# A mixture-of-experts diffusion block on one core: experts' results weighted at their eviction, residual tiles loaded ahead, layer 1's attention norm applied untransposed

## Chip, cores and metric

The kernel runs as one program on one core of a Trainium2 chip. The metric is the device time of one execution in microseconds. It is given as the median of three runs; the profile comes from one further execution.

## The reference, cut to what matters

Two layers work on 1024 latent tokens and 256 context tokens of width 1024, all in float32. Each layer has an attention part and a mixture of 32 experts, of which each token uses two. Only the parts that the change touches are shown.

```python
for i in range(DEPTH):                                   # 2 layers
    sh_a, sc_a, gt_a, sh_f, sc_f, gt_f = jnp.split(mod, 6, axis=-1)     # one row each for latents (modc for context)
    h  = _modulate(_rmsnorm(x, g_attn[i]), sh_a, sc_a)   # rmsnorm(x) * g * (1 + sc) + sh
    hc = _modulate(_rmsnorm(xc, g_attn[i]), shc_a, scc_a)
    q, k, v = _split_qkv(h, w_qkv[i])
...
    y = _hier_moe(tokens, ...)      # out[token] = sum over its 2 experts of w_buf * ((silu(xe @ w_gate) * (xe @ w_up)) @ w_down)
    x = x + gt_f * y[:b * n].reshape(b, n, d)
    if not last:
        xc = xc + gtc_f * y[b * n:].reshape(xc.shape)
return _rmsnorm(x, g_final)
```

In the last layer only the latents go through the experts.

## The kernel before, in words

Tokens are handled in tiles of 128, one token per partition: 8 latent tiles and 2 context tiles. Each layer runs in stages, one after another: `keys` (attention norm, keys and values), `queries`, attention (`attention` in layer 0, `dense` in layer 1), `project` (output projection, residual, second norm, routing) and `moe` (the experts). After layer 1 comes `final`. PE is TensorE, DVE is VectorE, ACT is ScalarE, POOL is GpSimd and SP is SyncE, which issues most DMAs.

Products are made in a split form: a float32 matrix becomes a high part (ACT copies it to a shorter type, L248 in `split`) and a low part (DVE subtracts, L249), and three products are added on PE (`mm3`, L280 to L282; `product`, L1330 to L1332).

**Experts.** `project` ends with the two weights of each token in `self.wts` (L1149, L1150) and with lists of tokens for each expert: `list0` has the first 128 tokens of each, `list1` the next 32 (`lists`, L1216). `moe` first queues gathers of the first two experts' tokens on POOL (L1419, L1421), then issues the remaining weight loads of expert 1 from POOL (L1424). Then it walks over 32 experts: gate and up products, SiLU, the turn of the hidden tile, and the down product into `py`. ACT evicts `py` plainly to the tile `yo` (L1472), and POOL scatters its rows to a DRAM buffer `y` (L1473), in which each token has two rows. `overflow` does the same for further tokens of a full expert, evicted at L1377, in branches of which some are taken. Within `moe` each engine issues in the order of the code (L1259).

**Combining.** `combine` (L380) takes one tile: SP loads the residual tile `x` (L384) and the two result rows of each token `y` (L386). ACT multiplies the first by its weight (L388), DVE multiplies the second by its weight and adds (L390), POOL multiplies by the gate row `gt` (L393), DVE adds the residual (L395). `keys` of layer 1 calls it for all 10 tiles, `final` for the 8 latent ones.

**Layer 1's keys.** Each tile passes `load` (combine), `norm`, `turn`, `product`, `post` and `turn_keys`; the loop at L526 emits them skewed, so that in step t tile t+3 is loaded, t+2 normed, t+1 turned and t multiplied. `norm` squares and sums on ACT (L430), takes the root on ACT and the reciprocal on DVE (`rstd`, L254 and L255), and scales the tile by it on DVE (L434). `turn` transposes on PE (L444). Then the norm's gain and shift are applied to the transposed tile, in which the model's width lies on partitions: four parts on DVE (L448) and four on ACT (L451), with scalars per partition from `vectors` (L359). The result `h` is split into `hl` (L455, L457). Outside `moe`, a scheduler orders the instructions of each engine from the order of the code and its own model of times; every engine then issues in that order, and an instruction that waits holds those behind it.

**Final.** For each latent tile: combine, squares and root as above, and one DVE operation that applies the reciprocal and the last norm's gain (L1484). SP stores it (L1485). The pool holds three tiles of `x` and of `y`.

Of the kernel before, what the change touches and what calls it, by code (L numbers as in the profile page):

```python
# [86 lines left out]
class Kernel:  # L87
# [13 lines left out]
    def run(self):  # L101
        with ExitStack() as ctx:
# [7 lines left out]
            self.y = [self.scratch(f"y{i}", [2 * NT * P, D], F32) for i in range(2)]  # L110
            self.lst = [self.scratch(f"lst{i}", [NT * P * NE, 4], I32) for i in range(2)]
# [8 lines left out]
    def consts(self):  # L120
# [70 lines left out]
        self.list1 = cp.tile([P, 2, NE], I32, name="list1")  # L191
# [188 lines left out]
    def combine(self, i, t, pool, gt):  # L380

        nc = self.nc
        x = pool.tile([P, D], F32, name="x", bufs=3)
        nc.sync.dma_start(x, self.x1[i][t * P:(t + 1) * P, :])  # L384
# [3 lines left out]
        nc.scalar.activation(y[:, 0, :], y[:, 0, :], AF.Copy, scale=self.wts[i][:, t, 0:1])  # L388
        yield
        nc.vector.scalar_tensor_tensor(y[:, 1, :], y[:, 1, :], self.wts[i][:, t, 1:2], y[:, 0, :],  # L390
                                       op0=OP.mult, op1=OP.add)
        yield
        nc.gpsimd.tensor_tensor(y[:, 1, :], y[:, 1, :], gt, op=OP.mult)  # L393
        yield
        nc.vector.tensor_tensor(x, x, y[:, 1, :], op=OP.add)  # L395
        return x

    def keys(self, i):
        nc, tc, A = self.nc, self.tc, self.A
        with ExitStack() as ctx:  # L400
# [4 lines left out]
            g1, sh = self.vectors(i, wp, ps)  # L405
            X, HL, PK, K2 = {}, {}, {}, {}
            if i:
                gk = self.bcast(wp, A["gk_b"][0], HD, "gk")
                gt = [self.bcast(wp, self.mod[0][v, 5 * D:6 * D], D, f"gt{v}") for v in range(2)]

            def load(t):
# [5 lines left out]
                else:  # L417
                    x = yield from self.combine(0, t, sb, gt[v])
# [5 lines left out]
            def norm(t):  # L424
# [9 lines left out]
                nc.vector.tensor_scalar(X[t], x, r, None, op0=OP.mult)  # L434
                yield

            def turn(t):
# [3 lines left out]
                h = sb.tile([P, KD, P], F32, name="h", bufs=1)  # L441
# [4 lines left out]
                for k in range(KD):  # L446
# [79 lines left out]
            for t in range(-3, NT + 2):  # L526
                if t == -1:
                    w = self.load_split(wp, st, A["w_qkv"][i][:, H * HD:], 2 * KV * HD, "wkv")
# [517 lines left out]
    def project(self, i):  # L1046
# [4 lines left out]
        with ExitStack() as ctx:  # L1051
# [98 lines left out]
            nc.vector.tensor_tensor(wt[:, :nt, 1:2], wt[:, :nt, 0:1], e[:, :, 4:5], op=OP.mult)  # L1150
            pc = ps.tile([P, NE], F32, name="pl", bufs=1)
# [64 lines left out]
    def lists(self, sb, plist, o, dst):  # L1216
# [8 lines left out]
        if o:  # L1225
            nc.vector.tensor_scalar(c[:, 2], c[:, 2], 4.0, self.quarter, op0=OP.mult, op1=OP.add)
# [20 lines left out]
    def moe(self, i):  # L1247
# [4 lines left out]
        with ExitStack() as ctx:  # L1252
# [142 lines left out]
            def overflow(e):  # L1395
# [18 lines left out]
                if e + 2 < NE:  # L1414
                    gather(xo[:, e % 2, :], list1[:32, 0, e + 2:e + 3])
# [92 lines left out]
```

## Time and profile before

| | |
|---|---|
| median of 3 runs | 3129.3 us (3125.08 to 3132.31) |
| profiled execution | 3136.02 us |
| its span, first to last instruction | 3134.2 us |
| mean granted TensorE clock | 0.951 |
| busy: PE, DVE, ACT, POOL | 2784.9, 2286.7, 1746.5, 711.8 us |

The profile is of one execution. Busy time counts an instruction from its start to its end, also while it waits for a port. An idle time is put down to what ended it. The experts of layer 0 run on PE from about 850 to 1505 us, those of layer 1 from about 2430 to 3059 us; layer 1's keys lie between 1506 and 1651 us, and `final` after 3059 us. The granted clock is a share of 2.4 GHz.

### The profile page before, as it was taken

The page shows a single profiled execution, that of the slowest core. Times are in us where ns is not written, and L with a number is a line of the kernel's source. Part 1 is how long each engine was busy: PE and PEld are TensorE (multiplying, and loading weights), DVE is VectorE, ACT ScalarE, POOL GpSimd, SP SyncE. Part 2 cuts the span into 40 slices and gives each one's busy share as a digit, 9 for nine tenths or more (in the row PEclk, how much of TensorE's full clock was granted, in tenths as well). Part 3 has the DMA queues.
Part 4 walks back from the last instruction along what each step waited for, and adds up shares of the span by engine and source line. Part 5 has one row for each costly group of instructions (what it writes and reads, how often), then busy time and mean ns, then how long its engine had stood idle before and what let it go on. Part 6 is the DMA issues. An engine that isn't in the chain of part 4 may idle for free. (4 is left out here: it accounts for less than half of the span.)

```text
span 3134.2 us, 43733 instructions
## 1 busy us (share of the span) xinstructions
PE 2784.9 (89%) x15685; PEld 2061.3 (66%) x15685; DVE 2286.7 (73%) x3159; ACT 1746.5 (56%) x2519; POOL 711.8 (23%) x436
## 2 busy tenths in 40 slices
PE   5999999989789999999578999999896999999990
PEld 3786555556578888888466744444475888888880
DVE  5564666666667888878585777777766787888885
ACT  4435666631266878877553433433421777778873
POOL 0110000011211111111232355656412211111112
PEclk8999999989899999999788999999998999999995
DMA  8466576062478989987745532212243888889956
GB/s 290 161 245 247 214 233 219 35 227 105 192 298 324 362 328 360 378 338 272 262 170 188 199 68 62 82 49 62 90 168 148 348 339 322 355 344 368 362 225 231
DMA packets 139959, 726.24 MB, mean 232 GB/s; under 512 B 32679, under 2 KB 32783, under 8 KB 69424
## 3 DMA queue, kind: packets, MB, share of 16 engines
q1 hardware_dynamic: 111808, 659.99, 55.9%
q0 software_dynamic: 24384, 56.68, 4.7%
q10 hardware_dynamic: 3376, 4.73, 0.4%
q8 instruction: 201, 3.29, 0.4%
q14 instruction: 190, 1.56, 0.1%
HBM read 628.65 MB, written 122.52 MB: 240 GB/s over the span
## 5 line engine op out<-in xcount | busy, mean ns | idle before, releaser
L249 DVE TENSOR_TENSOR whl<-raw,whl 128x1024 fp32r<-128x1024 f32 x560 | 661.1, 1221 | 62.8 <-ACT whl L248 59.1
L248 ACT ACTIVATE whl<-raw 128x1024 fp32r<-128x1024 f32 x560 | 574.2, 1057 | 40.0 <-DVE whl L249 14.0
L1330 PE MATMUL pup<-whl,xT 128*128 128x256 f32 x1024 | 291.3, 284 | 30.0 <-PEq L1397 26.5
L921 ACT ACTIVATE E<-T 128x1024 f32<-128x1024 f32 x160 | 163.8, 1024 | 232.8 <-PE T L919 232.8
L1331 PE MATMUL pup<-whl,xT 128*128 128x256 f32 x1024 | 285.0, 278 | 4.7 <-issue 4.6
L1332 PE MATMUL pup<-whl,xT 128*128 128x256 f32 x1024 | 285.2, 279 | 2.5 <-issue 2.5
L249 DVE TENSOR_TENSOR whl<-fq,whl 128x1024 fp32r<-128x1024 f32 x208 | 244.6, 1219 | 25.0 <-ACT whl L248 23.8
L908 DVE TENSOR_REDUCE mx<-S 128x1 f32<-128x1280 f32 x120 | 178.8, 1490 | 101.7 <-PE S L904 101.2
L248 ACT ACTIVATE whl<-fq 128x1024 fp32r<-128x1024 f32 x208 | 213.2, 1060 | 36.2 <-PE pgate L1332 16.8
L939 POOL TENSOR_TENSOR sum<-sum,E 128x1024 f32<-128x1024 f32 x77 | 189.8, 2465 | 179.9 <-ACT E L921 179.7
L1330 PEld LDWEIGHTS pup<-whl,xT 128*128 128x128 f32 x1024 | 193.2, 189 | 49.2 <-issue 46.5
L1330 PE MATMUL py<-whl,hT 128*128 128x512 f32 x512 | 205.0, 400 | 0.0
L1332 PE MATMUL pgate<-whl,xT 128*128 128x512 f32 x512 | 203.8, 398 | 0.1
L1330 PE MATMUL pgate<-whl,xT 128*128 128x512 f32 x512 | 201.5, 393 | 2.3 <-ACT xT L248 2.3
L1331 PE MATMUL pgate<-whl,xT 128*128 128x512 f32 x512 | 202.5, 396 | 0.0
L1332 PE MATMUL py<-whl,hT 128*128 128x512 f32 x512 | 201.6, 394 | 0.0
L1331 PE MATMUL py<-whl,hT 128*128 128x512 f32 x512 | 200.8, 392 | 0.0
L1088 POOL TENSOR_TENSOR hh<-hh,shf 128x1024 f32<-128x1024 f32 x18 | 43.5, 2415 | 687.2 <-DMA ot<-oT 425.7
L1332 PEld LDWEIGHTS pup<-whl,xT 128*128 128x128 f32 x1024 | 193.6, 189 | 5.1 <-issue 5.1
L1331 PEld LDWEIGHTS pup<-whl,xT 128*128 128x128 f32 x1024 | 193.4, 189 | 2.8
L777 ACT ACTIVATE PT<-pT 128x256 f32<-128x256 f32 (+1 forms) x288 | 118.4, 419 | 109.3 <-PE pT L768 105.9
L1293 POOL DMA_INDIRECT xo<-hf,list x64 | 85.7, 1339 | 400.3 <-PEq L1397 389.7
(316 smaller groups left out, 6662.9 us busy)
## 6 DMA issues: line engine op xcount, KB each, us to landing
raw<-in_w_down SPq DMA_DIRECT2D x100, 1024.0 KB
raw<-in_w_gate SPq DMA_DIRECT2D x86, 1024.0 KB
raw<-in_w_up SPq DMA_DIRECT2D x84, 1024.0 KB
wada<-in_w_ada SPq DMA_DIRECT2D x48, 1024.0 KB
fq<-in_w_gate SPq DMA_DIRECT2D x40, 1024.0 KB
fq<-in_w_up SPq DMA_DIRECT2D x40, 1024.0 KB
qT<-qt SPq DMA_DIRECT2D x31, 1024.0 KB
qt<-qT SPq DMA_DIRECT2D x27, 1024.0 KB
```

The costliest lines, as they stand in the source:

```text
L248: self.nc.scalar.activation(hi, src, AF.Copy)
L249: self.nc.vector.tensor_tensor(lo, src, hi.bitcast(F32), op=OP.subtract)
L777: nc.scalar.activation(dst, out[a][:, :hi - lo, :], AF.Copy)
L908: return lambda: nc.vector.tensor_reduce(MX[n][:, h:h + 1], S, axis=AX.X, op=OP.max, negate=True)
L921: nc.scalar.activation(E[n, j], b, AF.Exp)
L939: eng.tensor_tensor(w, SUM[n, who], E[n, j], op=OP.add)
L1088: nc.gpsimd.tensor_tensor(hh, hh, shf[v], op=OP.add)
L1293: nc.gpsimd.indirect_dma_start(out=dst, out_offset=None, in_=self.hf[i][0:nt * P, :], in_offset=bass.IndirectOffsetOnAxis(ap=idx, axis=0), ...
L1330: nc.tensor.matmul(out, lhsT=x[:, 0], rhs=w[:, 0, cols], start=first, stop=False)
L1331: nc.tensor.matmul(out, lhsT=x[:, 0], rhs=w[:, 1, cols], start=False, stop=False)
L1332: nc.tensor.matmul(out, lhsT=x[:, 1], rhs=w[:, 0, cols], start=False, stop=last)
```

## The change

Three things are changed.

1. The weights go to DRAM (`wd`, two per token) at the end of `project`. `moe` gathers them by the lists to `ws`, one per partition, for each expert, and the evictions of `py` multiply by them. `combine` then adds the two results on DVE, multiplies by the gate on POOL and adds the residual on DVE. `list1` gets a third column, the plain row of a token's result.
2. `keys` of layer 1 and `final` load residual tiles by themselves, before the results: three ahead in `keys`, all eight in `final`. `final` emits its tiles skewed, with four buffers of results, and ACT issues its stores.
3. In layer 1 the norm's gain and shift are broadcast rows. `norm` multiplies the tile by its reciprocal and the gain row in one DVE operation, and POOL adds the shift row. `turn` transposes that and splits straight from PSUM. Gate, gain and shift rows share one buffer each: rows for the latents first, those for the context loaded before tile 8. The weights `wkv` are loaded at the loop's first step.

```diff
@@ -108,6 +108,7 @@
             self.y = [self.scratch(f"y{i}", [2 * NT * P, D], F32) for i in range(2)]
+            self.wd = [self.scratch(f"wd{i}", [2 * NT * P, 1], F32) for i in range(2)]
             self.lst = [self.scratch(f"lst{i}", [NT * P * NE, 4], I32) for i in range(2)]
...
@@ -188,7 +189,7 @@
         self.list0 = cp.tile([P, 2, NE], I32, name="list0")
-        self.list1 = cp.tile([P, 2, NE], I32, name="list1")
+        self.list1 = cp.tile([P, 3, NE], I32, name="list1")
         self.pos = cp.tile([P, NT, 2], I32, name="pos")
...
@@ -377,23 +378,17 @@
-    def combine(self, i, t, pool, gt):
+    def combine(self, i, t, x, pool, gt):
...
         nc = self.nc
-        x = pool.tile([P, D], F32, name="x", bufs=3)
-        nc.sync.dma_start(x, self.x1[i][t * P:(t + 1) * P, :])
         y = pool.tile([P, 2, D], F32, name="y")
...
         yield
-        nc.scalar.activation(y[:, 0, :], y[:, 0, :], AF.Copy, scale=self.wts[i][:, t, 0:1])
+        nc.vector.tensor_tensor(y[:, 0, :], y[:, 0, :], y[:, 1, :], op=OP.add)
         yield
-        nc.vector.scalar_tensor_tensor(y[:, 1, :], y[:, 1, :], self.wts[i][:, t, 1:2], y[:, 0, :],
-                                       op0=OP.mult, op1=OP.add)
+        nc.gpsimd.tensor_tensor(y[:, 0, :], y[:, 0, :], gt, op=OP.mult)
         yield
-        nc.gpsimd.tensor_tensor(y[:, 1, :], y[:, 1, :], gt, op=OP.mult)
-        yield
-        nc.vector.tensor_tensor(x, x, y[:, 1, :], op=OP.add)
-        return x
+        nc.vector.tensor_tensor(x, x, y[:, 0, :], op=OP.add)
...
@@ -402,11 +397,29 @@
             ps = self.pool(ctx, f"kp{i}", 2, space=PSUM)
-            g1, sh = self.vectors(i, wp, ps)
             X, HL, PK, K2 = {}, {}, {}, {}
+
+            def first(t):
+                X[t] = xp.tile([P, D], F32, name="x")
+                nc.sync.dma_start(X[t], self.x1[0][t * P:(t + 1) * P, :])
+
             if i:
+                xp = self.pool(ctx, f"kx{i}", 3)
+                gt, g1, sh = {}, {}, {}
+                row = lambda j, v, c, name: self.bcast(wp, self.mod[j][v, c * D:(c + 1) * D], D, name)
+
+                def norm_rows(v):
+                    g1[v], sh[v] = row(i, v, 1, "g1"), row(i, v, 0, "sh")
+                    ga = self.bcast(st, A["g_attn"][i], D, "raw")
+                    nc.vector.scalar_tensor_tensor(g1[v], g1[v], 1.0, ga, op0=OP.add, op1=OP.mult)
+
+                gt[0] = row(0, 0, 5, "gt")
+                norm_rows(0)
                 gk = self.bcast(wp, A["gk_b"][0], HD, "gk")
-                gt = [self.bcast(wp, self.mod[0][v, 5 * D:6 * D], D, f"gt{v}") for v in range(2)]
+                for t in range(3):
+                    first(t)
+            else:
+                g1, sh = self.vectors(i, wp, ps)
...
@@ -415,7 +428,10 @@
                 else:
-                    x = yield from self.combine(0, t, sb, gt[v])
+                    if t not in X:
+                        first(t)
+                    x = X[t]
+                    yield from self.combine(0, t, x, sb, gt[v])
                     if not v:
...
@@ -431,19 +447,26 @@
                 yield
-                nc.vector.tensor_scalar(X[t], x, r, None, op0=OP.mult)
+                if not i:
+                    nc.vector.tensor_scalar(X[t], x, r, None, op0=OP.mult)
+                    yield
+                    return
+                v = int(t >= NLAT)
+                nc.vector.scalar_tensor_tensor(X[t], x, r, g1[v], op0=OP.mult, op1=OP.mult)
+                yield
+                nc.gpsimd.tensor_tensor(X[t], X[t], sh[v], op=OP.add)
                 yield
...
                 pt = ps.tile([P, KD, P], F32, name="pt")
-                h = sb.tile([P, KD, P], F32, name="h", bufs=1)
+                h = pt if i else sb.tile([P, KD, P], F32, name="h", bufs=1)
                 for b in (4, 0):
...
                 yield
-                for k in range(KD):
+                for k in range(0 if i else KD):
                     if k >= 4:
...
@@ -524,7 +547,11 @@
             for t in range(-3, NT + 2):
-                if t == -1:
+                if t + 3 == NLAT:
+                    gt[1] = row(0, 1, 5, "gt")
+                if t + 2 == NLAT:
+                    norm_rows(1)
+                if t == -3:
                     w = self.load_split(wp, st, A["w_qkv"][i][:, H * HD:], 2 * KV * HD, "wkv")
...
@@ -1148,6 +1175,7 @@
             nc.vector.tensor_tensor(wt[:, :nt, 1:2], wt[:, :nt, 0:1], e[:, :, 4:5], op=OP.mult)
+            nc.sync.dma_start(self.wd[i][0:2 * nt * P].rearrange("(t p k) o -> p t (k o)", p=P, k=2), wt[:, :nt])
             pc = ps.tile([P, NE], F32, name="pl", bufs=1)
...
@@ -1223,6 +1251,7 @@
         if o:
+            nc.vector.tensor_tensor(dst[:, 2], c[:, 2], gone, op=OP.add)
             nc.vector.tensor_scalar(c[:, 2], c[:, 2], 4.0, self.quarter, op0=OP.mult, op1=OP.add)
...
@@ -1267,6 +1296,9 @@
             xx = cs.tile([P, KD, 32], F32, name="xx")
+
+            ws = cs.tile([P, 2, 2], F32, name="ws")
+            nc.gpsimd.memset(ws, 0.0)
             hl, xT, pg, pt = {}, {}, {}, [None]
...
@@ -1294,6 +1326,12 @@
                     bounds_check=nt * P - 1, oob_is_err=False)
+
+            def weights(dst, idx):
+                nc.gpsimd.indirect_dma_start(
+                    out=dst, out_offset=None, in_=self.wd[i][0:2 * nt * P, :],
+                    in_offset=bass.IndirectOffsetOnAxis(ap=idx, axis=0),
+                    bounds_check=2 * nt * P - 1, oob_is_err=False)
...
@@ -1374,7 +1412,7 @@
                 yo = sb.tile([P, D // 4], F32, name="yoo", bufs=1)
-                nc.scalar.activation(yo, py, AF.Copy)
+                nc.scalar.activation(yo, py, AF.Copy, scale=ws[:, 1, e % 2:e % 2 + 1])
                 nc.gpsimd.indirect_dma_start(
...
@@ -1407,18 +1445,24 @@
                             nc.vector.tensor_scalar(l2[:, 1:2], rows, self.quarter, None, op0=OP.add)
+                            nc.vector.tensor_scalar(l2[:, 2:3], rows, 0.25, None, op0=OP.mult)
                             gather(xo[:, e % 2, :], l2[:32, 0:1])
+                            weights(ws[:, 1, e % 2:e % 2 + 1], l2[:, 2:3])
                             late_tokens(e)
...
                     gather(xo[:, e % 2, :], list1[:32, 0, e + 2:e + 3])
+                    weights(ws[:, 1, e % 2:e % 2 + 1], list1[:, 2, e + 2:e + 3])
                 pump()
...
                 gather(xo[:, e, :], list1[:32, 0, e:e + 1])
+            for e in range(2):
+                weights(ws[:, 0, e:e + 1], list0[:, 1, e:e + 1])
+                weights(ws[:, 1, e:e + 1], list1[:, 2, e:e + 1])
             for c in range(6):
...
@@ -1469,20 +1513,45 @@
                 yo = self.qp.tile([P, D], F32, name="q")
-                nc.scalar.activation(yo, py, AF.Copy)
+                nc.scalar.activation(yo, py, AF.Copy, scale=ws[:, 0, e % 2:e % 2 + 1])
                 scatter(yo, list0[:, 1, e:e + 1])
+                if e + 2 < NE:
+                    weights(ws[:, 0, e % 2:e % 2 + 1], list0[:, 1, e + 2:e + 3])
                 ahead()
...
         nc, tc, A = self.nc, self.tc, self.A
-        with tc.tile_pool(name="fw", bufs=1) as wp, tc.tile_pool(name="fb", bufs=3) as sb:
+        with tc.tile_pool(name="fx", bufs=NLAT) as xp, tc.tile_pool(name="fw", bufs=1) as wp, \
+                tc.tile_pool(name="fb", bufs=4) as sb:
+            X = []
+            for t in range(NLAT):
+                X.append(xp.tile([P, D], F32, name="x"))
+                nc.sync.dma_start(X[t], self.x1[1][t * P:(t + 1) * P, :])
             gt = self.bcast(wp, self.mod[1][0, 5 * D:6 * D], D, "gt")
             gf = self.bcast(wp, A["g_final"], D, "gf")
-            for t in range(NLAT):
-                x = run(self.combine(1, t, sb, gt))
-                r = self.row_rstd(sb, x)
+
+            def tile(t):
+                x = X[t]
+                yield from self.combine(1, t, x, sb, gt)
+                yield
+                junk = sb.tile([P, D], BF16, name="junk", bufs=1)
+                ss = sb.tile([P, 1], F32, name="ss")
+                nc.scalar.activation(junk, x, AF.Square, accum_out=ss)
+                yield
+                r = self.rstd(sb, ss, D, 1, "rstd")
+                yield
                 nc.vector.scalar_tensor_tensor(x, x, r, gf, op0=OP.mult, op1=OP.mult)
-                nc.sync.dma_start(self.out[0, t * P:(t + 1) * P, :], x)
+                nc.scalar.dma_start(self.out[0, t * P:(t + 1) * P, :], x)
+
+            waiting, going = [tile(t) for t in range(NLAT)], []
+            while waiting or going:
+                going += waiting[:1]
+                del waiting[:1]
+                for g in list(going):
+                    for _ in range(2):
+                        if next(g, self) is self:
+                            going.remove(g)
+                            break
...
```

## Rows read from the trace of the kernel before

**Rows 1.** Section 1 of the page: each engine's busy time, its share of the span and its instructions.
```profile
PE 2784.9 (89%) x15685; PEld 2061.3 (66%) x15685; DVE 2286.7 (73%) x3159; ACT 1746.5 (56%) x2519; POOL 711.8 (23%) x436
```

**Rows 2.** The table by stage: stretch in us from the span's start, its length, then for PE, PE's weight loads, DVE, ACT and POOL the busy us and the instructions, then the granted clock, the mean busy share of the 16 DMA engines and GB/s.
```profile
960.00:1500.00 540.00, 519.77 (x3277) 454.08 (x3276) 454.98 (x471) 409.01 (x466) 95.63 (x80) 0.99 0.84 332
1518.00:1560.00 42.00, 18.66 (x71) 14.79 (x72) 27.03 (x37) 26.12 (x43) 11.94 (x7) 0.64 0.89 332
1560.00:1630.00 70.00, 53.29 (x254) 41.69 (x253) 65.08 (x113) 43.02 (x93) 29.55 (x24) 0.88 0.59 224
1630.00:1645.00 15.00, 12.87 (x67) 9.84 (x65) 10.11 (x27) 6.95 (x17) 3.89 (x5) 1.00 0.00 1
1518.00:1645.00 127.00, 84.82 (x388) 66.32 (x388) 102.22 (x175) 76.09 (x151) 45.39 (x35) 0.81 0.62 233
3075.00:3131.00 56.00, 0.00 (x0) 0.00 (x0) 37.38 (x32) 21.17 (x33) 19.66 (x8) 0.50 0.68 236
```

**Rows 3.** The timeline of DVE and POOL in layer 1's keys and in `final`: start and duration in us, engine, line, operation, out<-in, shapes, how many (merged where they follow one another), and in brackets the idle time before and what ended it.
```profile
1585.86 1.21 DVE L457 TENSOR_TENSOR hl<-h,hl 128x1024 fp32r<-128x1024 f32 x1
...
1597.85 0.74 DVE L434 TENSOR_SCALAR xn<-x,rstd 128x1024 f32<-128x1024 f32 x1
...
1603.82 1.36 DVE L448 TENSOR_SCALAR h<-pt,g,sh 128x128 f32<-128x128 f32 x4
...
1603.97 2.39 POOL L393 TENSOR_TENSOR y<-y,gt 128x1024 f32<-128x1024 f32 x1 [1.17 <-DVE y L390]
...
1608.71 3.36 DVE L457 TENSOR_TENSOR hl<-h,hl 128x1024 fp32r<-128x1024 f32 x1
...
1608.54 2.45 POOL L393 TENSOR_TENSOR y<-y,gt 128x1024 f32<-128x1024 f32 x1 [1.43 <-DVE y L390]
...
3087.31 2.47 DVE L390 SCALAR_TENSOR_TENSOR y<-y,wts 128x1024 f32<-128x1024 f32 x2
...
3097.87 3.44 DVE L1484 SCALAR_TENSOR_TENSOR x<-x,rstd,gf 128x1024 f32<-128x1024 f32 x1
...
3097.89 2.34 POOL L393 TENSOR_TENSOR y<-y,gt 128x1024 f32<-128x1024 f32 x1 [3.61 <-DVE rstd L255]
...
3106.21 2.50 DVE L395 TENSOR_TENSOR x<-x,y 128x1024 f32<-128x1024 f32 x2 [2.32 <-DMA x<-x]
...
3129.10 1.28 DVE L1484 SCALAR_TENSOR_TENSOR x<-x,rstd,gf 128x1024 f32<-128x1024 f32 x1
```

**Rows 4.** The same view among the experts, DVE.
```profile
871.28 4.62 DVE L249 TENSOR_TENSOR whl<-raw,whl 128x1024 fp32r<-128x1024 f32 x4
```

**Rows 5.** Groups of instructions in layer 1's keys, 1517 to 1646 us, DVE then ACT: line, engine, operation, out<-in, shapes and count, then busy us and mean ns of one, then the engine's idle time before them and what ended it.
```profile
L448 DVE TENSOR_SCALAR h<-pt,g,sh 128x128 f32<-128x128 f32 x40 | 14.1, 401 | 6.5 <-ACT h L451 6.4
L390 DVE SCALAR_TENSOR_TENSOR y<-y,wts 128x1024 f32<-128x1024 f32 x10 | 13.5, 1350 | 3.6 <-ACT y L388 3.6
...
L451 ACT ACTIVATE h<-pt,sh,g 128x128 f32<-128x128 f32 x40 | 15.4, 454 | 9.2 <-PE pt L444 4.5 <-DVE k L486 3.2 <-DVE rstdh L255 1.4
L388 ACT ACTIVATE y<-y,wts 128x1024 f32<-128x1024 f32 x10 | 11.4, 1150 | 5.6 <-DMA y<-y 4.2 <-DVE y L390 1.3
...
L248 ACT ACTIVATE wq<-raw 128x1024 fp32r<-128x1024 f32 x4 | 4.2, 1052 | 0.0
```

**Rows 6.** The timeline at the start of layer 1's keys: SP, ACT and PE.
```profile
1513.03 0.80 SPq L386 DMA_DIRECT2D y<-y  x2
...
1518.13 1.15 ACT L388 ACTIVATE y<-y,wts 128x1024 f32<-128x1024 f32 x1 [4.25 <-DMA y<-y]
...
1539.99 0.80 PE L280 MATMUL pk<-wkv,hl 128*128 128x512 f32 x1 [6.70 <-ACT hl L455]
```

**Rows 7.** The chain of waits that ended last, in `final`: start, duration, what.
```profile
3070.03 4.81 DMA y<-y
...
3101.73 4.40 DMA x<-x
...
3119.16 5.07 DMA x<-x
```

**Rows 8.** The start of DVE's work in `final` in its timeline, and ACT's groups of 3074 to 3131 us.
```profile
3076.10 1.28 DVE L390 SCALAR_TENSOR_TENSOR y<-y,wts 128x1024 f32<-128x1024 f32 x1 [16.38 <-ACT y L388]
...
L262 ACT ACTIVATE junk<-x 128x1024 bf16<-128x1024 f32 x8 | 8.4, 1052 | 16.9 <-DVE x L395 16.9
L254 ACT ACTIVATE rstd<-ss,eps 128x1 f32<-128x1 f32 x8 | 2.3, 291 | 0.2
L262 ACT ACTIVATION_READ_ACCUMULATOR junk<-x 128x1 f32 x8 | 1.5, 186 | 0.0
```

**Rows 9.** The table by stretch before the first results of `final` land, columns as in group 2.
```profile
3065.00:3067.00 2.00, 0.00 (x0) 0.00 (x0) 0.00 (x0) 0.00 (x0) 0.97 (x1) 1.00 1.02 416
...
3069.00:3071.00 2.00, 0.00 (x0) 0.00 (x0) 0.00 (x0) 0.00 (x0) 0.00 (x0) 0.50 0.13 41
```

**Rows 10.** The timeline where layer 0's experts start: DVE, POOL and ACT.
```profile
838.28 0.16 DVE L1150 TENSOR_TENSOR wts<-wts,e 128x10 f32<-128x10 f32 x1
...
847.84 1.95 POOL L1293 DMA_INDIRECT xo<-hf,list  x1 [0.30 <-issue]
849.79 0.60 POOL L1244 DMA_DIRECT2D raw<-in_w_gate  x1
...
869.99 4.06 ACT L248 ACTIVATE whl<-raw 128x1024 fp32r<-128x1024 f32 x4
```

## The prediction, made blind

> **What bounds the kernel now.** I read the busy shares first: PE 89%, VectorE (DVE) 73%, ScalarE (ACT) 56%, GpSimd (POOL) 23% [rows 1]. These are averages, and the change lies in three stages, so the table by stage comes next [rows 2]. In the expert stage (960 to 1500) PE is busy 519.8 of 540 us: PE sets the time, and ACT (409.0) and POOL (95.6) have room. In layer 1's key stage (1518 to 1645) PE has 84.8 of 127 us; from 1560 to 1630 DVE is busy 65.1 of 70. In the last stage (3075 to 3131) PE does nothing, and DVE and POOL have 37.4 and 19.7 of 56 us.
>
> Then the timeline of DVE and POOL beside each other [rows 3]. A POOL addition or multiplication and a DVE operation on two SBUF tensors don't run together. POOL multiplies from 1608.54 for 2.45 us; a DVE subtraction that takes 1.21 us alone begins at 1608.71 and takes 3.36. At 3097.87 the same happens to an L1484 (3.44 for 1.28, POOL at 3097.89). Four L448 operations, which read PSUM and per-partition scalars, run beside POOL's 2.39 us at 1603.97 in their usual 1.36. So a busy DVE contains waits for POOL, and in the key stage and the last stage DVE and POOL are nearly one resource: what either takes on two SBUF tensors, the other loses.
>
> The Trainium skill states this in "SBUF — State Buffer", section "SBUF: two separate sides": the two engines share one port pair as an exclusive lock, against DVE operations with two SBUF inputs or in a two-port mode. The trace agrees (3.36 us for 1.21). By that rule the low part of a tile, read from PSUM after the change, leaves the lock too: some 10 x 1.2 us, so the lock's load would rise by about 17 us rather than the total of both engines by 15 below.
>
> **The change part by part.** Durations are of this execution: 3136.02 us, its span 3134.2, and 6.7 above the median 3129.3 of the runs shown; I carry differences over to the median.
>
> *Layer 1's keys, the joint load of DVE and POOL*, per stage of 10 tiles. Added: POOL's shift, 10 x 2.34 (L393 at 3097.89 [rows 3]) = +23.4. L434 (0.74 at 1597.85) becomes a product of two tensors and a scalar, as L390 is (two in 2.47, 1.24 each [rows 3]): 10 x 0.5 = +5. The product that makes the second g1 row +1.2; the first lies before the first results land. L390 becomes an addition of 1.16 (four L249 in 4.62 [rows 4]): 10 x -0.08 = -0.8. Removed: the DVE half of the transposed scale and shift, 40 L448, four in 1.36 = -13.6. Sum +15.2. Some L448 had lain under POOL (the four at 1603.82), so taking them away returns less; the low part read from PSUM may take that place. I let these two cancel. Bounds: all ten low parts under POOL -11; all L448 hidden before +13.
>
> *What is given back.* DVE idled 6.4 us before L448 for ACT's half and 3.6 before L390 for ACT's scaling [rows 5]; both operations go from ACT (15.4 and 11.4 us), so up to 10 us. Other waits move up: the norm's root and reciprocal, and turning, which now follows a POOL operation. I take 5. Startup: results issued at 1513.03 reach ACT at 1518.13; PE makes the stage's first product at 1539.99 [rows 6]. Without the ACT step (1.15) and the transposed one (some 3 us, four ACT parts and four DVE parts) the first product comes some 6 us earlier, but with an added 2.34 us of POOL; this shortens the wait before the joint resource is full and is part of the 5.
>
> *Queues of this stage.* Gate, scale, shift and norm rows are 512 KB broadcasts: two before, eight now. Two more come before the first tile: 1.05 MB at 332 GB/s, the rate of 1518 to 1560 [rows 2], are 3.2 us of transfers, partly while experts still run; I put 0 to 2 us on the first result. The context rows reuse their buffers: the SP queue waits for POOL's last latent multiplication, and the next results stand behind it. Two tiles already loaded and PE's backlog cover that; uncovered it would be one landing, 4.8 us [rows 7]. Weights of wkv are issued earlier and were waited for little. No end is moved away: PE follows this stage with the queries, so its end is the program's. Keys: 15.2 - 5 = **+10**, from -3 (low parts hidden, 8 given back) to +20 (nothing given back, hidden L448 lost).
>
> *Last stage.* Per tile now 1.24 + 2.34 + 1.25 (two L395 in 2.50) + 0.1 + 1.24 = 6.2 [rows 3, 8]; after, 1.16 replaces the first 1.24: 6.1, for 8 tiles 48.7. The reciprocal's 0.1 is its share when the pipe is full. DVE works from 3076.10 to 3130.38, 54.3 us, so 5 us are idle: residual tiles that came late, 4.40 and 5.07 us in the chain [rows 7]. With all eight loaded ahead these waits go; late next is the tail of the last tile, ACT's square and root (1.05 + 0.19 + 0.29 [rows 8]), and hand-overs, together 2.5: 51.2 us. But the first result comes later. Five more residual tiles, 2.6 MB at 416 GB/s [rows 9], lie in the same SP queue ahead of it, 6.3 us; the queue was empty only just before (41 GB/s after 3069). So transfers end near 3075.3 instead of 3069, and the first result's 1 MB (2.5 us) lands at 3077.8, not 3074.84. ACT's 1.15 is gone, so DVE begins at 3077.8 rather than 3076.10: +1.7. Together 1.7 + 51.2 - 54.3 = -1.4; the last scatter competes with the transfers too, but ACT now issues the stores, which frees SP. I take **-2** (bounds -7, if results overtake the residuals, and +2).
>
> *Experts.* Scaling at the eviction costs ACT about 0.1 us (1150 against 1052 ns for plain [rows 5]) in 64 evictions, hidden under PE but for the last of each layer: +0.2. Each expert adds two gathers of 4-byte weights on POOL, which had 95.6 of 540 us; at most 1.95 us each, as a row gather at the start took [rows 10]: some 29 experts x 2 x 1.95 = 113 us more, still under half of the stage. Behind them wait scatters and token gathers, needed an expert later. At each start, four gathers go in front of the POOL-issued loads of expert 1 (849.79): 4 x 2.2 = 8.8 us later. Their first split among expert 1's is at 869.99 or later [rows 10], so 11 us remain for the first chunk; cost 0 to 5. Writing the weights to DRAM is one SP issue with 8-byte pieces, which no row shows; it ends before POOL's turn if it takes under 11 us (weights ready at 838.44, POOL's turn at 849.79 [rows 10]). Between 0 and 5; I take **+0.5** for all, nearest the rows with slack.
>
> Sum: +10 - 2 + 0.5 = +8.5; rounded down for the tail of the key stage, where DVE has room (10.1 of 15 [rows 2]), **+8**: 3144 for the profiled execution, **3137** as median.
>
> **The rivals.** *Faster, latency sets the key stage.* Before DVE fills up, each tile passes ACT, DVE, POOL, DVE, ACT, DVE, PE; two stations are dropped, and the startup's 6 us and the 10 us of DVE waits come back in full while low parts run under POOL (-11 of the 15.2). For it: DVE has only 27.0 of 42 us up to 1560. Against it: 65.1 of 70 after. It decides from the point where the returned waits and overlap exceed 15.2. Keys -6, last stage -5: 3118. Chance 0.20.
> *No difference.* Half the added POOL time finds DVE waiting or on PSUM (-8): keys +3, last stage -2: 3130. Chance 0.25.
> *Experts starve at the start.* The 8.8 us on POOL, or SP held by the write until the weights are ready, pass on to PE: +5 in each layer on top of the keys: 3147. Against it: 11 us of slack. Chance 0.07.
> *It doesn't load ahead.* If results wait behind eight residual tiles, the last stage gains nothing: this is inside the -2.
>
> **How the numbers follow.** The forecast, slower by about 8, has 0.48. About 0.2% (6.3 us) is what a measurement can tell from no change. Slower: 0.07 plus most of the forecast, 0.41 + 0.07 = 0.48; the forecast's low part 0.07 and the second rival give same 0.32; faster 0.20. The range takes keys -3 to +20, last stage -7 to +2, experts 0 to +5: 3119 to 3156, cut to **3119 to 3154**. The forecast's own range is 3134 to 3148.
>
> **What would show it.** Right: POOL busy in the key stage up from 45 to near 69 us, DVE operations stretched to over 3 us more often, DVE near full from 1540 on, the stage some 10 us longer though L448 and L451 are gone; the last stage without residual waits, its first addition near 3077 plus the shift; PE unchanged among the experts. Wrong: a key stage no longer than 127 us, low parts mostly inside POOL's time, or first results that land before the residual tiles.

## The result and the profile after

Five runs of the changed kernel have a median of 3157.9 us (3155.3 to 3166.6), five of the kernel before on the same chip 3132.3. The ratio is **1.0091, 95% interval 1.0071 to 1.0111**: slower by 22 to 35 us. The forecast had the sign (slower) and a third of the size (+8); its range ended at 3154. Ratios here and below leave out three single executions that took far longer than the others (3969 us of the kernel before, 13631 of e2, 4970 of e6). The profiled execution took 3155.28 us, its span 3153.6, at the same mean clock as before (0.951).

The first row of the page, answering [rows 1]:

```profile
PE 2785.9 (88%) x15684; PEld 2061.6 (65%) x15684; DVE 2283.6 (72%) x3118; ACT 1719.1 (55%) x2461; POOL 906.2 (29%) x576
```

PE's work is the same; what was added are waits. To find them I cut each trace by PE's own landmarks (the last matmul of the router's lists, of the last expert's product and of the transposes of layer 1's keys, and the end of the span), in us:

| Stretch | before | after | difference | forecast |
|---|---|---|---|---|
| start to the first router's end | 839.4 | 836.1 | -3.3 | 0 |
| experts, layer 0 | 665.6 | 676.2 | **+10.6** | +0.5 for both layers |
| layer 1's keys | 146.2 | 154.6 | **+8.4** | +10 |
| queries to the second router's end | 767.0 | 764.7 | -2.3 | 0 |
| experts, layer 1 | 645.0 | 652.6 | **+7.6** | (with layer 0) |
| last stage | 71.0 | 69.4 | -1.6 | -2 |

The four changed stretches sum to +25.0, about the difference of the medians (25.6); the two profiled executions as a whole differ by 19.4. The two unchanged ones wander: over the thirteen profiled executions of this study the first lay between 834.3 and 843.5 and the other between 762.1 and 770.2. So single stretches are compared below, and totals only where runs carry an interval.

**Where the experts lose.** The timeline of SyncE's queue (SP) around the router's end of layer 0, before (start, duration, instruction):

```profile
822.05 0.32 SPq L1089 DMA_DIRECT2D hf<-hh  x1
822.46 1.20 SPq L1244 DMA_DIRECT2D raw<-in_w_down  x2
823.72 1.70 SPq L1244 DMA_DIRECT2D raw<-in_w_gate  x3
839.64 0.34 SPq L1244 DMA_DIRECT2D raw<-in_w_up  x1
```

and after:

```profile
818.67 0.32 SPq L1116 DMA_DIRECT2D hf<-hh  x1
835.09 0.37 SPq L1178 DMA_DIRECT2D wd<-wts  x1
835.51 1.88 SPq L1273 DMA_DIRECT2D raw<-in_w_down  x2
837.43 4.09 SPq L1273 DMA_DIRECT2D raw<-in_w_gate  x3
```

The longest wait of that queue after, from the table of waits (us in total, times, longest):

```profile
SPq L1178 <- DVE wts L1177: 16.0, 1, 16.0
```

The new write `wd<-wts` stands in SyncE's queue and waits 16.0 us for the weights. Five loads of 1 MB had gone out right behind the last `hf` store; now they stand behind the write (the expectations below say six; the sixth, `in_w_up`, stands in both kernels behind SyncE's read of the number of overfull lists, which the router's last step writes, and goes out after the router's end: 839.64 before, 842.77 after). The table by stage shows the hole (stretch, its length, busy us of PE, PEld, DVE, ACT and POOL with counts, clock, share of the DMA engines, GB/s). Before:

```profile
820.00:840.00 20.00, 9.99 (x115) 7.45 (x114) 13.85 (x77) 2.97 (x4) 3.99 (x3) 0.62 0.73 290
840.00:860.00 20.00, 12.35 (x48) 9.77 (x49) 13.54 (x17) 9.84 (x11) 11.41 (x10) 0.61 0.71 262
860.00:880.00 20.00, 17.15 (x98) 14.79 (x98) 15.36 (x17) 14.89 (x18) 4.20 (x4) 1.00 0.96 380
```

After:

```profile
820.00:840.00 20.00, 8.65 (x110) 6.14 (x108) 13.14 (x80) 6.33 (x8) 3.52 (x5) 0.59 0.16 23
840.00:860.00 20.00, 8.94 (x26) 6.65 (x27) 8.22 (x8) 3.80 (x4) 11.62 (x12) 0.53 0.96 372
860.00:880.00 20.00, 15.17 (x81) 13.29 (x80) 12.08 (x13) 10.52 (x12) 1.50 (x2) 0.74 1.01 416
```

From 820 to 840 the DMA engines move 23 GB/s instead of 290; then they are full. The gather of expert 0's tokens (`xg`) now lands among the weights, as I read its longer wait. PE's longest wait there, before and after:

```profile
PE pt L1312 <- DMA xg<-hf,list: 6.7, 1, 6.7
```

```profile
PE pt L1350 <- DMA xg<-hf,list: 13.5, 1, 13.5
```

The first expert's gate (its Silu on ACT, counted from the table load before it) comes 26.7 us after the router's end instead of 20.0, the second's another 26.5 later instead of 21.3; from there to the last expert's it is 611.2 us against 612.4. So the whole loss lies at the start of the stage. In layer 1 the numbers are 25.8 for 21.6 and 24.4 for 22.3, which is 6.3 of the 7.6 us.

**The keys.** VectorE's and GpSimd's groups from 1525 to 1660 (busy us, mean ns, idle before them):

```profile
L391 DVE TENSOR_TENSOR x<-x,y 128x1024 f32<-128x1024 f32 x10 | 18.4, 1836 | 11.0 <-POOL y L389 11.0
L387 DVE TENSOR_TENSOR y<-y 128x1024 f32<-128x1024 f32 x10 | 17.5, 1746 | 2.9 <-DMA y<-y 2.9
...
L455 DVE SCALAR_TENSOR_TENSOR xn<-x,rstd,g 128x1024 f32<-128x1024 f32 x10 | 15.3, 1531 | 0.8 <-PE pt L467 0.6
L480 DVE TENSOR_TENSOR hl<-pt,hl 128x1024 fp32r<-128x1024 f32 x10 | 12.1, 1207 | 0.2 <-ACT hl L478 0.2
```

```profile
L389 POOL TENSOR_TENSOR y<-y,gt 128x1024 f32<-128x1024 f32 x10 | 26.8, 2678 | 30.4 <-DMA raw<-in_w_qkv 15.7 <-DVE y L387 5.6 <-DVE rstd L256 5.4
L457 POOL TENSOR_TENSOR xn<-xn,sh 128x1024 f32<-128x1024 f32 x10 | 24.6, 2462 | 15.0 <-DVE xn L455 9.2 <-DVE rstdh L256 3.3 <-DMA raw<-in_w_qkv 2.5
```

GpSimd's shift costs 24.6 us, and the additions of two SBUF tensors, 1.2 us each when alone, now take 1.75 to 1.84 on the mean. The low part, which reads PSUM, is never stretched (1207 ns; before, from SBUF, ten had a mean of 1628, and two took 3.20 and the 3.36 of [rows 3]).

The stage also gets going later. The first transposes come 32.9 us after the last expert product (before: 26.3), and from there to its end it is 121.7 us against 119.9. The first results are asked for 8.7 us after the last scatter instead of 6.2. In front of them in SyncE's queue stand two loads of `wkv`, and the second waits for VectorE's product of the gain row, which frees the buffer that it takes:

```profile
SPq L273 <- DVE g L414: 6.3, 1, 6.3
```

In e4 (below), which has no gain row, the interval is 7.5 us.

**The last stage**, its first instructions, answering [rows 7, 8]:

```profile
3086.05 1.00 POOL L1337 DMA_INDIRECT y<-q,list  x1 [17.54 <-DMA x<-x]
3094.11 12.21 SPq L385 DMA_DIRECT2D y<-y  x5
3101.02 1.22 DVE L387 TENSOR_TENSOR y<-y 128x1024 f32<-128x1024 f32 x1 [20.38 <-DMA y<-y]
...
3147.71 1.29 DVE L1543 SCALAR_TENSOR_TENSOR x<-x,rstd,gf 128x1024 f32<-128x1024 f32 x1
```

From the last scatter to the first loads of results it is now 8.1 us (before: 5.0, from 3065.04 to 3070.03), and VectorE then needs 48.0 us instead of 54.3, with no wait for a residual left.

### The profile page after: what moved, and what is told of

Same layout as the page of the kernel before. It is cut to its first block, busy times and chain, and to the rows that moved or that the text cites. A ratio compares the mean times of both kernels' runs of the same rounds, so it can differ in the third digit from the quotient of the medians.

```text
span 3153.6 us, 43869 instructions
## 1 busy us (share of the span) xinstructions
PE 2785.9 (88%) x15684; PEld 2061.6 (65%) x15684; DVE 2283.6 (72%) x3118; ACT 1719.1 (55%) x2461; POOL 906.2 (29%) x576
## 5 line engine op out<-in xcount | busy, mean ns | idle before, releaser
L250 DVE TENSOR_TENSOR whl<-fq,whl 128x1024 fp32r<-128x1024 f32 x208 | 244.1, 1220 | 25.6 <-ACT whl L249 23.7
L1337 POOL DMA_INDIRECT y<-q,list x64 | 77.7, 1214 | 383.9 <-ACT q L1516 364.0
```

The source lines that it names most:

```text
L250: self.nc.vector.tensor_tensor(lo, src, hi.bitcast(F32), op=OP.subtract)
L1337: return nc.gpsimd.indirect_dma_start(out=self.y[i][0:2 * nt * P, :], out_offset=bass.IndirectOffsetOnAxis(ap=idx, axis=0), in_=src, in_of ...
```

## The experiments

Stage lengths are those of the table above, from one profiled execution each. Where the code of a stage is the same they differ by up to about 2.5 us (experts of layer 1: 652.2 to 654.7 in the changed kernel, e4, e6, e7, e8 and e9; keys: 141.8 in e4 and 139.1 in e10), so smaller differences decide nothing. Ratios are against the kernel before on the same chip.

| Run | experts 0 | keys | experts 1 | last stage | ratio, 95% interval |
|---|---|---|---|---|---|
| before | 665.6 | 146.2 | 645.0 | 71.0 | |
| changed | 676.2 | 154.6 | 652.6 | 69.4 | 1.0091, 1.0071 to 1.0111 |
| e1 | 668.9 | 155.3 | 650.8 | 70.1 | 1.0048, 1.0031 to 1.0065 |
| e2 | 671.5 | 146.4 | 651.8 | 70.3 | 1.0046, 1.0026 to 1.0067 |
| e3 | 673.1 | 154.8 | 651.0 | 70.7 | 1.0078, 1.0062 to 1.0095 |
| e5 | 666.3 | 155.6 | 646.0 | 70.4 | 1.0040, 1.0024 to 1.0056 |
| e4 | 676.5 | 141.8 | 652.6 | 69.4 | 1.0034, 1.0023 to 1.0044 |
| e6 | 677.0 | 145.0 | 654.0 | 70.1 | 1.0059, 1.0042 to 1.0076 |
| e8 | 676.4 | 149.5 | 654.3 | 70.3 | 1.0082, 1.0055 to 1.0108 |
| e9 | 675.5 | 155.0 | 654.7 | 69.4 | 1.0085, 1.0064 to 1.0105 |
| e7 | 675.8 | 153.8 | 652.2 | 68.1 | 1.0098, 1.0075 to 1.0121 |
| e10 | 666.1 | 139.1 | 647.3 | 64.1 | 0.9965, 0.9953 to 0.9977 |
| e11 | 666.1 | 144.4 | 646.3 | 68.3 | 0.9986, 0.9975 to 0.9998 |

**e1, e2, e3 and e5: the start of the experts.** e1:

```diff
-            nc.sync.dma_start(self.wd[i][0:2 * nt * P].rearrange("(t p k) o -> p t (k o)", p=P, k=2), wt[:, :nt])
+            nc.scalar.dma_start(self.wd[i][0:2 * nt * P].rearrange("(t p k) o -> p t (k o)", p=P, k=2), wt[:, :nt])
```

> The changed kernel with one edit: the weights' write to DRAM is issued by ScalarE, not by SyncE. Theory H (the hold): on SyncE the write waits 16.0 us for the weights and six expert loads of 1 MB stand behind it (issued from 835.51 after, from 822.46 before). Then the first gathers and loads come early again, and the time from the last router product to the last expert product falls from 676.8 to about 667 us in layer 0 and from 653.2 to about 646 in layer 1 (before: 666.2 and 645.6); total 14 to 18 us below the changed kernel, near 3142. Rival P (GpSimd's queue): four more gathers in front of expert 1's loads set the start; then the stages stay within 4 us of 676.8 and 653.2 and the total near 3156.

e2 puts the same write, on SyncE, into the kernel before:

```diff
...
+            nc.sync.dma_start(self.wd[i][0:2 * nt * P].rearrange("(t p k) o -> p t (k o)", p=P, k=2), wt[:, :nt])
```

> The kernel before with one addition: the weights are written to DRAM by SyncE at the place where the change writes them; nobody reads them, all else is as before. H: six expert loads are issued some 13 us later, and the kernel before becomes 12 to 18 us slower (about 3147), its expert stages about 676 and 652 us. P: nothing but a small write is added, 0 to 2 us (3130 to 3133), expert stages 666 and 646.

e3 moves the start's gathers:

```diff
+            for c in range(6):
+                if (1, c) not in raw:
+                    self.load_expert(i, 1, c, nc.gpsimd)
             for e in range(2):
                 weights(ws[:, 0, e:e + 1], list0[:, 1, e:e + 1])
                 weights(ws[:, 1, e:e + 1], list1[:, 2, e:e + 1])
-            for c in range(6):
-                if (1, c) not in raw:
-                    self.load_expert(i, 1, c, nc.gpsimd)
```

> The changed kernel with the four weight gathers at the start of each expert stage moved behind GpSimd's loads of expert 1; the write stays on SyncE. H: the hold remains, so the total stays within 4 us of the changed kernel (3154 to 3160). P: the loads of expert 1 start about 5 us earlier (four gathers of 1.0 us at a spacing of 1.3), and the two stages together get 6 to 14 us shorter (3144 to 3152).

e5 has both edits.

> The changed kernel with both edits: ScalarE issues the weights' write, and the four weight gathers at the start stand behind GpSimd's loads of expert 1. If hold and GpSimd's queue are the two causes, each for its own part (with the write moved alone the expert stages were 668.9 and 650.8 us, with the gathers late alone 673.1 and 651.0, before 665.6 and 645.0), both gains come: 665 to 668 and 645 to 648 us. Rival W (the write itself: 8-byte pieces in the DMA engines just ahead of the token gathers): the first token transposes stay some 3 us behind those of before in layer 0 (10.6 us after the router's end with the write moved, 6.9 before), and the stages stay at 668 to 670 and 648 to 650.

Measured: the write alone, read by nobody, costs the kernel before 5.9 and 6.8 us in its two expert stages (ratio 1.0046, 8 to 21 us). The total and layer 1 are as H said; layer 0 loses about half of the 10 us that H had for it. Taking the hold out of the changed kernel (e1) returns 7.3 us in layer 0, as H said, but only 1.8 in layer 1, where H expected 7 and which is P's figure; the total falls by 10 us by the medians and 13 by the ratios, less than H's 14 to 18. Moving the gathers alone (e3) returns 3.1 and 1.6, less than P's least. Both together (e5) give everything back: 9.9 and 6.6. So there are two causes. In layer 0 they add up (7.3 and 3.1 one by one, 9.9 together). In layer 1 they hide each other (1.8 and 1.6 one by one, 6.6 together): there either one alone leaves the second expert late. Its gate comes 24.4 us after the first's in the changed kernel, 25.4 with the write moved, 24.4 with the gathers late, 20.7 with both (before 22.3). The totals of e1 and e5 (1.0048 and 1.0040) don't tell these two apart; this rests on the stage lengths. The queue of SyncE in e5 is that of before again:

```profile
816.89 0.32 SPq L1116 DMA_DIRECT2D hf<-hh  x1
817.26 1.25 SPq L1273 DMA_DIRECT2D raw<-in_w_down  x2
818.56 1.64 SPq L1273 DMA_DIRECT2D raw<-in_w_gate  x3
```

and PE's first wait there:

```profile
PE pt L1350 <- DMA xg<-hf,list: 10.3, 1, 10.3
```

That is 3.6 us more than before (6.7), the delay that W named; but the second expert makes it up in layer 0 (19.7 us after the first, before 21.3), and W's stage lengths were not met. Whether the write's small pieces make this delay no run here separates: it stays open, and with 0.7 and 1.0 us left over in the two stages it decides nothing. The scaled evictions and the gathers inside the stages, which e5 has too, lie within the same 1 us.

**e4, e6, e8 and e9: the keys.** e4 takes the norm of before back (the transposed scale and shift too, and no norm rows):

```diff
...
-                nc.vector.scalar_tensor_tensor(X[t], x, r, g1[v], op0=OP.mult, op1=OP.mult)
-                yield
-                nc.gpsimd.tensor_tensor(X[t], X[t], sh[v], op=OP.add)
+                nc.vector.tensor_scalar(X[t], x, r, None, op0=OP.mult)
...
```

> The changed kernel with the norm of layer 1's keys as before (scale and shift per partition after the transpose, no shift on GpSimd, no norm rows); weights at the eviction and residuals ahead stay. Theory J (joint load of VectorE and GpSimd): that load falls by 10 x 2.34 + 10 x 0.5 + 1.2 - 13.6 = 16 us; the stretch from the last expert product to the keys' last transpose falls from 154.5 to 138 to 146 us (before: 146.2), total 8 to 16 us less than the changed kernel (3142 to 3150). Rival S (the start: rows loaded ahead of the results, a second pass through GpSimd before the first product): the start gives back 4 us at most and the rest stays: 150 to 154 us, total 3153 to 3158.

e6 keeps the new norm and moves one addition:

```diff
-                nc.gpsimd.tensor_tensor(X[t], X[t], sh[v], op=OP.add)
+                nc.vector.tensor_tensor(X[t], X[t], sh[v], op=OP.add)
```

> The changed kernel with one edit: the shift of layer 1's normalised keys input is added by VectorE (about 1.2 us) instead of GpSimd (2.34). J (joint load): ten times 1.1 us less, the stretch from the last expert product to the keys' last transpose falls from 154.6 to 143 to 149 us. Rival V (VectorE alone is the bound): ten times 1.2 us more on VectorE, 156 to 166 us. Rival S (the start): 152 to 155.

e8 and e9 add one addition per tile to e4, whose result nobody reads. This is e9's; e8 has the first gate row as both inputs:

```diff
...
+                    more = sb.tile([P, D], F32, name="more", bufs=1)
+                    nc.gpsimd.tensor_tensor(more, X[t], gt[int(t >= NLAT)], op=OP.add)
```

> The kernel with the norm of before (stretch of the keys 141.8 us) plus one GpSimd addition of 128x1024 per tile, on the gate row, whose result nobody reads: it only costs GpSimd 10 x 2.34 us. J: VectorE waits while GpSimd adds, so the stretch grows by 10 to 20 us, to 152 to 162. Rival L (the way through GpSimd is what counts, since each tile waits for its own shift): nobody waits for this addition and the stretch stays at 141 to 146.

> As the run with idle additions, but each addition reads its own tile's normalised x, so that the ten lie spread over the stage (in that run they all ran at its start, 24 us in one piece, so it priced a late start and no load). Nobody reads the results; GpSimd's 10 x 2.34 us is all that is added to the kernel with the norm of before (141.8 us). J: the stretch grows by 8 to 20 us, to 150 to 162. Rival L (only the way through GpSimd counts): 141 to 146.

e4's stretch is 141.8 us, e6's 145.0: J's figures, and V and S fall. In e6 VectorE makes the ten shifts itself (13.4 us), and still its busy time in the stretch falls from 113.6 to 106.2 and the stretch by 9.6: what GpSimd does not do, VectorE does not wait for. L would also explain this, since a pass through GpSimd is gone. e8 was a poor test of it: all ten additions ran at once at the start (24.0 us in one piece, the first transposes 8.8 us later), so I read its +7.7 us as the price of a late start. e9 mends that: the first transposes come no later (27.8 us after the last expert product, e4: 28.5) and the stretch is 155.0 us, **13.2 more** for 10 additions whose results nobody waits for. The table by stage, e4 and e9 (columns as above):

```profile
1520.10:1661.90 141.80, 85.46 (x403) 66.21 (x401) 99.03 (x187) 70.58 (x149) 48.00 (x37) 0.77 0.60 227
```

```profile
1509.80:1664.80 155.00, 89.41 (x403) 68.97 (x401) 116.39 (x187) 71.09 (x149) 77.51 (x47) 0.77 0.57 208
```

VectorE has the same 187 instructions and is busy 17.4 us longer with them, while its idle time falls from 42.8 to 38.6. So it is not kept waiting for something behind GpSimd: its own operations are stretched. J is shown, L falls. Where the time goes, in e9's groups of the stretch:

```profile
L469 DVE TENSOR_TENSOR hl<-h,hl 128x1024 fp32r<-128x1024 f32 x10 | 16.5, 1653 | 1.9 <-ACT hl L467 1.9
```

```profile
L446 POOL TENSOR_TENSOR more<-xn,gt 128x1024 f32<-128x1024 f32 x10 | 28.2, 2824 | 18.3 <-DVE xn L443 18.3
```

against e4's same subtraction:

```profile
L466 DVE TENSOR_TENSOR hl<-h,hl 128x1024 fp32r<-128x1024 f32 x10 | 12.2, 1218 | 0.8 <-ACT hl L464 0.8
```

The ten subtractions from SBUF take 4.3 of the 17.4 us more; other operations of VectorE share the rest.

No run separates one part of the change: `wkv` is loaded at the first step in the changed kernel and in every run but e2. What e4 has below the kernel before (146.2 to 141.8) is this, the residuals and the weighting together.

**e7, e10 and e11: the residuals, and a faster kernel.** e7:

```diff
-            for t in range(NLAT):
+
+            def first(t):
                 X.append(xp.tile([P, D], F32, name="x"))
                 nc.sync.dma_start(X[t], self.x1[1][t * P:(t + 1) * P, :])
+
+            for t in range(2):
+                first(t)
...
+                if t + 2 < NLAT:
+                    first(t + 2)
                 yield from self.combine(1, t, x, sb, gt)
```

> The changed kernel with one edit in the last stage: three residual tiles are loaded ahead of the first results and each later one two tiles ahead of its use, instead of all eight first. If five tiles too many stand before the first results, the first addition comes about 4 us earlier (12.4 instead of 16.3 us after the last expert product) and the stage takes 65 to 67 us (69.4 after, 71.0 before). Rival: the later residuals are late again, as in the kernel before, and the stage stays at 69 to 71 us.

The stage takes 68.1 us, between the two. The edit did not do what I meant: the scheduler moved one more residual ahead, so that four, not three, were issued before the first results, and the time from the scatter to them was not shortened (8.3 us). e10 therefore writes SyncE's order of the last stage by hand, results first, and mends all else:

> The changed kernel with four parts mended: the write by ScalarE, the start's weight gathers late, the keys' norm as before, and in the last stage two residual tiles ahead of the first results and each later one behind the results of an earlier tile. From the stages measured: experts 666.3 and 646.0, keys 141.8, last stage 65 to 68 (before: 665.6, 645.0, 146.2, 71.0): 6 to 9 us below the kernel before, 3121 to 3126 at a median of 3130. If the parts don't add up (the keys' gain lost as the experts end elsewhere, or the last stage at 70), 3127 to 3133.

```profile
3061.66 1.00 POOL L1321 DMA_INDIRECT y<-q,list  x1 [17.67 <-ACT q L1500]
3066.36 0.32 SPq L385 DMA_DIRECT2D y<-y  x1
3066.73 0.42 SPq L1516 DMA_DIRECT2D x<-x  x1
...
3071.26 1.22 DVE L387 TENSOR_TENSOR y<-y 128x1024 f32<-128x1024 f32 x1 [15.01 <-DMA y<-y]
```

Scatter to first results is 4.7 us, and the first addition comes 11.0 us after the last expert product (changed kernel 16.4, before 12.4). The stage takes 64.1 us. The parts add up, to somewhat more than I had put down for them: e10 is **faster than both kernels**, 3120.9 us, ratio 0.9965 (0.9953 to 0.9977).

e11 keeps the old weighting and has e10's residuals, order and norm:

> The kernel before with only the residual tiles ahead (three ahead in layer 1's keys; in the last stage two ahead of the first results, and its two tiles interleaved as in the change); weights stay in the sum of the results, no write, no weight gathers, the keys' norm as before. If the gain of the mended kernel comes from the residuals, this has nearly all of it: experts 665.6 and 645.0, keys 142 to 145, last stage 67 to 69, total 3123 to 3128. If it comes from ScalarE's weighting step that is dropped, keys 145 to 147, last stage 69 to 71, total 3127 to 3133.

Its stages (144.4 and 68.3) lie within the first case, its time (3127.9 us) within both, but what the first case says falls, since e10 gained more than I had put down for it: e11 has 0.9986 (0.9975 to 0.9998), less than half of e10's gain. The two differ by 5.3 us in the keys and 4.2 in the last stage, and by 7.0 in their medians. So the weighting at the eviction, once its weights are fetched without harm, is worth some 7 us and the rest, the residuals ahead above all, some 4; the intervals are too wide to say which is worth more.

## Why the prediction was wrong

**Experts: the step that failed.** I costed them at +0.5 (0 to +5); measured +18.2 in the two layers. The failing sentence is that the write "ends before POOL's turn if it takes under 11 us". It asked who waits for the write's result, GpSimd, and not what stands behind the write in SyncE's own queue: five loads of 1 MB, which before went out at 822.46 to 825.4, some 13 us ahead of the weights. e2 shows that wait alone (5.9 and 6.8). The rival "experts starve at the start" named this very wait, but I set its price at 5 a layer and its chance at 0.07 against "11 us of slack", a slack of GpSimd's queue and not of SyncE's. Its mechanism with 10.6 and 7.6 in place of 5 and 5 is the result. The other half of that step, four gathers that delay GpSimd's loads, was taken as nearly covered too. Measured, first to first, these loads begin 14.6 us after the router's end instead of 10.4, a delay of 4.2 where I had 8.8; yet it costs 3.1 and 1.6 us beside the hold (e3) and 2.6 and 4.8 without it (e1 against e5). The 11 us of slack ran from a load's issue to its first split, and the load's own landing had to fit in there too. What I said of the evictions and gathers inside the stage (hidden) holds: e10, which has them, has 666.1 and 647.3, and e11, which has not, 666.1 and 646.3.

**Keys: right in sum, in part by luck.** +10 forecast, +8.4 measured. The joint load of VectorE and GpSimd is shown (e9, and e6 agrees), but two steps of the sum were off and cancelled. The load is smaller than its terms: the new norm costs 12.8 in all (154.6 against e4's 141.8), of which 4.4 lie before the first transposes (32.9 against 28.5) and 8.4 behind them, where my terms for it were 23.4 + 5 + 1.2 - 13.6 = 16. The measured price of an addition that nobody waits for is 1.32 us of the stage for 2.34 of GpSimd (13.2 over ten), so 0.56 of it and not all. And the startup, which I had some 4 us shorter (6 less 2.34), is 6.6 longer, so that of the +8.4 only 1.8 lie behind the first transposes: the first results are asked for later, behind a load that waits 6.3 us for the gain row, a hold in SyncE's queue as among the experts, and the norm passes GpSimd once more. What comes with the new norm gives back 4.4 (146.2 to 141.8), where I took 5 + 0.8. Of the signs named, GpSimd's busy time in the stretch rose as said (47.1 to 72.2), and five operations of VectorE took over 3 us where two had; VectorE was not near full (83.8 of 95 us from 1545 to 1640).

The low parts, read from PSUM, are not stretched at all, ten of 1207 ns; I had let what this saves cancel against something else. On this the Trainium skill ("SBUF — State Buffer", section "SBUF: two separate sides") was the better guide: it names two SBUF inputs as what meets the lock. e9 agrees too, where the scale and shift that reads PSUM keeps its 398 ns a piece (e4: 401) and the subtraction from SBUF grows to 1653. Its sum was 17 us of load where mine was 15; neither is the stage's loss.

**Last stage: right in sum, by two errors.** -2 forecast, -1.6 measured. The first addition came 16.4 us after the last expert product; I had 14.1 (3077.8). The missing 2.3 is the scatter, 3.1 us longer to its readers beside the eight residual loads: I named that competition and gave it nothing. VectorE then took 48.0 us, where I had 51.2: the tiles follow each other every 5.79 us (3141.05 after 3135.26 on GpSimd) and not every 6.1. The residual waits are gone, as said.

**The range.** It held keys at up to +20 and the experts at +5, and so ended 4 us under the measured median. With the measured values in their places the same three terms give 18.2 + 8.4 - 1.6 = 25.0, about the measured difference: no stage was missing from the sum, one was mispriced.

## What to carry to other kernels

A DMA that waits for a computed value must not stand in an in-order queue ahead of loads that need nothing: give it to the engine that is idle when the value is ready, and read off what is queued behind it, not only who wants its result. Moving an elementwise addition from VectorE to GpSimd did not free VectorE here, where both read two SBUF tensors: an addition on VectorE (1.2 us) was cheaper for the stage than one on GpSimd (2.34). Prefetch as much as the next two steps need: what goes beyond that moves beside the transfer that sets the start (here two residual tiles ahead against eight: 4.7 us from the scatter to its first reader against 8.1). And ask of every load put into the queue early what it waits for itself: the second `wkv` load held the first results for a row that VectorE had yet to make.

## What the runs showed that was not expected

Two delays at one place need not add, and the same two can do either: mending one of them returned 7.3 or 3.1 us in layer 0 and 1.8 or 1.6 in layer 1, mending both 9.9 and 6.6. So in layer 0 the gains add, and in layer 1 each alone is no more than that stage varies by. That there the later of two sets of loads sets the second expert's start is my reading; no run shows when the loads land.

A scatter of 512 KB followed by its readers took 4.7 us (e10) with two residual tiles issued shortly before it and 5.0 with three (before), and 8.1 with eight (changed kernel); with four (e7) it took as long as with eight, 8.3. So the number of tiles alone does not decide it.

Stretches in which nothing was changed differ by up to 9 us between profiled executions (834.3 to 843.5 to the first router's end). In one of these places, from 660 to 680, the granted clock was 0.83 in the kernel before and 1.00 after; no run shows that this makes the difference. A total from one execution can therefore hide or feign a third of this change; the lengths of the changed stages agree to 1 to 2.5 us where nothing differs (keys 154.6, 155.3, 154.8, 155.6 and 153.8 in the changed kernel, e1, e3, e5 and e7).
